# Rotary exchanges issued by ScalarE instead of SyncE, and the solve's plain blocks recorded ahead of the transposed ones, in a two-layer hybrid decoder trunk

## The chip, the cores and the metric

One core of one Trainium2 chip. The metric is device time in microseconds; lower is better. PE is TensorE, DVE is VectorE, ACT is ScalarE, POOL is GpSimd, SP is SyncE; SPq is the sequence in which SP issues DMAs.

## The reference

Two layers over 512 tokens of width 1024. Each layer has a token mixer of four head groups that read one normalised input through one combined projection, then cross-attention into 256 memory tokens, then a SwiGLU FFN. Two of the head groups matter here:

```python
def rotary(x, cos, sin):
    half = x.shape[-1] // 2
    x1, x2 = x[..., :half], x[..., half:]
    ...
    return jnp.concatenate([x1 * c - x2 * s, x1 * s + x2 * c], axis=-1)

# retention group
qh = rotary(heads(q), cos, sin)
kh = rotary(heads(k), cos, sin) * (HEAD_DIM ** -0.5)

# RWKV-7 group, per token
sa = jnp.einsum('bhvk,bhk->bhv', state, -kk_t)
state = (state * w_t[:, :, None, :] + sa[..., None] * (kk_t * a_t)[:, :, None, :]
         + v_t[..., None] * k_t[:, :, None, :])
```

The kernel takes the RWKV recurrence 64 tokens at a time, which needs the inverse of a unit triangular 64x64 matrix for each head and each 64 tokens.

## The kernel before

Channels lie on the partitions and the 512 tokens along the free dimension. Every large product is done with a high and a low part of each operand: a weight block of 1024x128 is loaded by SP into one of three buffers `u`, ACT rounds it into `v` (CAST v<-u), DVE takes the rest into `w` (w<-u,v), and PE makes 24 matmuls of 128x128 by 128x512 into an accumulator `a`. These are called dense matmuls below. All other products go into the five PSUM tiles `b`. SBUF tiles `s` are 128x512, there are 71; `z` and `q` are smaller tiles of the RWKV scan. `fd` and `nd` are tensors in DRAM.

**What sets the order.** The program is first only recorded. `Sched.record` notes each operation with its operands, and links it to what it depends on; `Sched.order` then simulates the five engines with a table of costs (`Sched.cost`: a DMA that SP or ACT issues holds its engine 470 ns) and takes, again and again, the operation that can start first, with ties broken by class and by the length of the chain behind it. The instructions are issued in that order, so each engine has a fixed sequence, and the waits are semaphores. The trace gives all operations line 564, the line in `Sched.issue` that calls them, so places are named by tiles. Moving a DMA to another engine, or recording it earlier, lets the planner come to another order for all that follows.

**The solve** (`rwkv_solve`, one per layer). POOL inverts the 32x32 diagonal blocks by substitution into `rf`, with one block per partition. ACT then makes a transposed copy: `A.copy(rt, rf.rearrange("p t w -> p w t"))`. Both are stored to DRAM (`fd..0` from `rt`, `fd..1` from `rf`; two DMAs each), and read back by 16 DMAs of 32 KB into four block-diagonal tiles: two from `rf` (called TT, one for each pair of heads) and two from `rt` (called R). `rwkv_whole` then makes the 64x64 inverses for each pair: 16 small matmuls of 64x64 with TT, a mask on DVE (two halves, `s<-b,cst`), 16 small matmuls with R, and a sum on DVE that puts the result in R. After both pairs, the scan over eight pieces of 64 tokens begins; its first product with R is the row `b<-z,s`.

**The rotary exchanges** (`retention`). Four projections per layer, q and k of two head pairs each, are rotated. For each, ACT copies the accumulator to `c`; four DMAs of 32x512 exchange neighbouring groups of 32 partitions from `c` into `s`; DVE multiplies the accumulator by the cosines into `t`, multiplies `s` by the sines and adds the two:

```python
A.copy(c, ps)
for b in range(4):
    o = 32 * (b ^ 1)
    self.Q.dma_start(s[o:o + 32], c[32 * b:32 * b + 32])
V.tensor_tensor(t, ps, rot[0], op=ALU.mult)
V.tensor_tensor(s, s, rot[1], op=ALU.mult)
V.tensor_tensor(t, t, s, op=ALU.add)
```

`self.Q` is SP. In the trace the exchange is `s<-s` on SPq. The solve and the rotary are independent of each other, and the planner interleaves both with the projections, the SSD group and later the RWKV scan.

Of the kernel before, what the change touches and what calls it, by code (L numbers as in the profile page):

```python
# [566 lines left out]
class Trunk:  # L567
# [468 lines left out]
    def retention(self, l, proj, vals):  # L1036
        V, A, E, G = self.V, self.A, self.E, self.G
        ident = self.con("ident")
        rot = []
        for i in range(2):  # L1040
            t = self.S()
            self.Q.dma_start(t, self.a["rot"][i])
            rot.append(t)
        qk = []
        for which in range(2):
            for i in range(2):
                ps = proj(COL_B + 256 * which + i * P)
                t, s, c = self.S(), self.S(), self.S()
                A.copy(c, ps)
                for b in range(4):  # L1050
                    o = 32 * (b ^ 1)
                    self.Q.dma_start(s[o:o + 32], c[32 * b:32 * b + 32])
                V.tensor_tensor(t, ps, rot[0], op=ALU.mult)
                V.tensor_tensor(s, s, rot[1], op=ALU.mult)
                V.tensor_tensor(t, t, s, op=ALU.add)
                qk.append(t)
        q, k = qk[0:2], qk[2:4]
        yt = rot
        st = None
        for j in range(4):  # L1060
            tk = slice(j * P, (j + 1) * P)
            v, ks = vals[j], self.S()
            b = self.bank()
            for i in range(2):
                E.transpose(b[:, i * P:(i + 1) * P], k[i][:, tk], ident)
            V.tensor_tensor(ks[:, 0:256], b[:, 0:256], self.con("retw"), op=ALU.mult)
            m = self.S()
            m4 = m.rearrange("p (i o t) -> p i o t", i=2, o=2)
            for o in range(2):
                b = self.bank()  # L1070
                rows = slice(HD * o, HD * o + HD)
                for i in range(2):
                    E.matmul(b[:, i * P:(i + 1) * P], k[i][rows, tk], q[i][rows, tk], start=True, stop=True)
                V.tensor_tensor(m4[:, :, o], b[:, 0:256].rearrange("p (i t) -> p i t", i=2),
                                self.con("retd").rearrange("p (i o t) -> p i o t", i=2, o=2)[:, :, o], op=ALU.mult)
            if j:
                for i in range(2):
                    V.tensor_tensor(q[i][:, tk], q[i][:, tk], self.con("retq")[:, i * P:(i + 1) * P], op=ALU.mult)
            yb = self.bank()
            for i in range(2):  # L1080
                if j:
                    E.matmul(yb[:, i * P:(i + 1) * P], q[i][:, tk], st[:, i * P:(i + 1) * P], start=True, stop=False, skip_group_check=True)
                for h in (2 * i, 2 * i + 1):
                    E.matmul(yb[:, h * HD:(h + 1) * HD], m[:, h * P:(h + 1) * P], v[:, h * HD:(h + 1) * HD],
                             start=(j == 0), stop=True, skip_group_check=True)
            A.copy(yt[j // 2][:, j % 2 * 256:(j % 2 + 1) * 256], yb[:, 0:256])
            if j < 3:

                for i in range(2):
                    E.matmul(yb[:, (2 + i) * P:(3 + i) * P], ks[:, i * P:(i + 1) * P], v[:, i * P:(i + 1) * P], start=True, stop=True)  # L1090
                new = ks[:, 256:512]
                V.tensor_tensor(new.rearrange("p (i c) -> p i c", i=2), yb[:, 256:512].rearrange("p (i c) -> p i c", i=2),
                                self.con("bones").unsqueeze(1).to_broadcast([P, 2, P]), op=ALU.mult)
                if j:
                    for i in range(2):
                        hs = slice(i * P, (i + 1) * P)
                        V.scalar_tensor_tensor(new[:, hs], st[:, hs], self.con("retg")[:, i:i + 1], new[:, hs], op0=ALU.mult, op1=ALU.add)
                st = new
        for t in yt:
            self.head_norm(t, 1e-5)  # L1100
        yy = []
        for i in range(2):
            b = self.bank()
            for j in range(4):
                E.transpose(b[:, j * P:(j + 1) * P], yt[j // 2][:, j % 2 * 256 + i * P:j % 2 * 256 + (i + 1) * P], ident)
            A.activation(k[i], b, AF.Identity, bias=self.par("ret_gn_b", l, i), scale=self.par("ret_gn_w", l, i))
            yy.append(k[i])
        return yy
# [103 lines left out]
    def rwkv_solve(self, l, nd):  # L1212


        V, A, G = self.V, self.A, self.G
        B, H = 32, 16
        nf = self.s.tile("n").rearrange("p (s t) -> p s t", s=B)
        rf = self.S().rearrange("p (t w) -> p t w", w=H)
        room = nf.rearrange("p s t -> p (s t)")
        rt = room[:, 0:B * H].rearrange("p (w t) -> p w t", t=B)  # L1220
        blk = [(self.rows(e).start + B * kb, e * HD + B * kb, B * kb) for e in range(2) for kb in range(HD // B)]
        for c2 in range(2):
            for m, (p0, x0, c0) in enumerate(blk):
                f0 = HD * c2 + 16 * m
                self.Q.dma_start(nf[f0:f0 + 16], nd[p0:p0 + B, :, x0:x0 + B].rearrange("s n t -> n s t"))
        flat = rf.rearrange("p t w -> p (t w)")
        G.memset(flat, 0.0)
        for c2 in range(2):
            G.memset(flat[HD * c2:HD * c2 + HD, H * c2:B * H:2 * H + 1], 1.0)
        for s in range(B - 1):  # L1230
            a, w = B - 1 - s, s // 2 + 1

            p0 = 0 if s else B * (B - 1)
            p3 = room[:, p0:p0 + a * w].rearrange("p (a w) -> p a w", a=a)
            G.tensor_tensor(p3, nf[:, s, s + 1:].unsqueeze(2).to_broadcast([P, a, w]),
                            rf[:, s, 0:w].unsqueeze(1).to_broadcast([P, a, w]), op=ALU.mult)
            done = G.tensor_tensor(rf[:, s + 1:, 0:w], rf[:, s + 1:, 0:w], p3, op=ALU.add)
        A.copy(rt, rf.rearrange("p t w -> p w t"))
        res = [[], []]
        for k, f in enumerate((rt, rf)):  # L1240
            fd = self.s.scratch([HD, B, B], f"fd{l}{k}", True)
            for c2 in range(2):
                half = fd.rearrange("f (w c) t -> f w c t", c=2)[:, :, c2] if k == 0 else fd[:, :, H * c2:H * c2 + H]
                self.Q.dma_start(half, f[HD * c2:HD * c2 + HD])
            for i in range(2):
                t = self.S()
                self.s.link(done, V.memset(t, 0.0), False)
                t3 = t.rearrange("p (n x) -> p n x", n=8)
                for m, (p0, x0, c0) in enumerate(blk):
                    f0 = 16 * m + 8 * i  # L1250
                    self.Q.dma_start(t3[p0:p0 + B, :, c0:c0 + B], fd[f0:f0 + 8].rearrange("n s t -> s n t"))
                res[i].append(t)
        self.solved = done
        return res

    @staticmethod
    def rows(e):
# [456 lines left out]
```

## Time and profile before

| | before |
|---|---|
| median of 3 runs | 1683.56 us (1681.34 to 1685.95) |
| the profiled execution, device time | 1683.98 us |
| its span, first to last instruction | 1682.1 us |
| PE busy | 1643.6 us (98%) |
| DVE busy | 1015.1 us (60%) |
| ACT busy | 633.2 us (38%) |
| mean granted clock of TensorE | 0.992 |

The span is split in the profile into 40 slices of 42 us; PE is at nine tenths or more in nearly all of them, and the slices that are not lie at the start, around 160 us, around 980 us, and at the end. The two in the middle are the solves of the two layers. A timeline row merges neighbouring like instructions: start, length, engine, operation, operands, count, and in brackets the idle time before it and what ended that. A granted clock of 1.00 is 2.4 GHz, one of 0.50 is 1.2 GHz.

### The profile page before, as it was taken

To read this page: it belongs to the slowest core of one execution; us is meant where nothing else is said; L and a number is where in the kernel's file an instruction comes from. 1 tells how busy PE (TensorE), PEld (TensorE's weight loads), DVE (VectorE), ACT (ScalarE), POOL (GpSimd) and SP (SyncE) were. 2 spreads that over 40 slices of the span, in tenths; PEclk is the share of its full clock that TensorE was granted. 3 is DMA by queue.
4 is the path that set the end of the run, shared out by engine and by line. 5 is a ranking of instruction groups with operands and counts; after the bars stand their busy time and mean duration, and the time that the engine had idled before them with its cause. 6 is when DMAs were issued, how large, how long until landed. Compare 5 with 4: busy or idle time off the path is not lost.

```text
span 1682.1 us, 21417 instructions
## 1 busy us (share of the span) xinstructions
PE 1643.6 (98%) x8344; PEld 1344.0 (80%) x8344; DVE 1015.1 (60%) x1796; ACT 633.2 (38%) x966; POOL 69.6 (4%) x140
## 2 busy tenths in 40 slices
PE   7998999999999999999999989999999999999997
PEld 7786778888788888888888867888888888888886
DVE  8867689666564545533477666986655655554333
ACT  7433246444442322322354332554444323232221
POOL 0043000000000000000000700000000000000001
PEclk9999999999999999999999999999999999999998
DMA  9345112632323333333453431145233333333331
GB/s 287 103 101 126 26 45 81 189 94 66 97 88 99 89 100 90 95 104 114 131 175 101 107 83 45 51 126 162 64 88 88 100 89 99 93 96 94 92 97 57
DMA packets 312900, 169.48 MB, mean 101 GB/s; under 512 B 35936, under 2 KB 300384, under 8 KB 312672
## 3 DMA queue, kind: packets, MB, share of 16 engines
q1 hardware_dynamic: 312800, 168.12, 34.8%
q8 instruction: 66, 1.08, 0.3%
q14 instruction: 34, 0.28, 0.1%
HBM read 156.56 MB, written 9.44 MB: 99 GB/s over the span
## 4 chain that ended last, share of the span: by engine, by line
PE 91%; DVE 4%; DMA 2%; ACT 2%; SPq 1%; issue 1%; DVEq 0%; ACTq 0%
PE a L564 81%; PE b L564 9%; DVE s L564 2%; ACT s L564 1%; DMA s<-s 1%; DVE w L564 1%; SPq L564 1%; ACT v L564 1%; DMA s<-in_lora_dram 0%; DMA s<-fd 0%; DMA s<-in_memT_dram 0%; DVE q L564 0%; DVE t L564 0%; DVEq L1710 0%; DVE z L564 0%
## 5 line engine op out<-in xcount | busy, mean ns | idle before, releaser
L564 PE MATMUL a<-s,v 128*128 128x512 f32 (+1 forms) x4012 | 1234.0, 388 | 7.6 <-ACT s L564 5.9
L564 PEld LDWEIGHTS a<-s,v 128*128 128x128 f32 x4012 | 743.8, 189 | 168.2 <-ACT s L564 6.5
L564 PE MATMUL a<-s,w 128*128 128x512 f32 (+1 forms) x2006 | 777.2, 387 | 0.5 <-DVE w L564 0.5
L564 ACT CAST v<-u 128x1024 fp32r<-128x1024 f32 (+3 forms) x275 | 282.4, 1027 | 673.6 <-PE a L564 384.4
L564 PEld LDWEIGHTS a<-s,w 128*128 128x128 f32 x2006 | 378.8, 189 | 80.0 <-issue 0.9
L564 DVE TENSOR_TENSOR w<-u,v 128x1024 fp32r<-128x1024 f32 (+3 forms) x275 | 329.2, 1198 | 169.5 <-ACT v L564 168.8
L564 DVE TENSOR_TENSOR s<-a,s 128x512 f32<-128x512 f32 (+1 forms) x132 | 90.5, 689 | 264.1 <-PE a L564 244.9
L564 ACT ACTIVATE s<-s 128x512 f32<-128x512 f32 (+3 forms) x233 | 144.7, 628 | 111.9 <-DVE s L564 107.3
L564 PE MATMUL b<-s,s 64*64 64x64 f32 (+8 forms) x1268 | 146.0, 275 | 14.8 <-DVE s L564 9.2
L564 DVE TENSOR_TENSOR s<-s,s 128x512 f32<-128x512 f32 (+4 forms) x223 | 139.9, 636 | 30.8 <-DMA s<-s 16.2
L564 PEld LDWEIGHTS b<-s,s 128*128 128x128 f32 (+3 forms) x1268 | 120.9, 171 | 42.9 <-issue 17.3
L564 DVE SCALAR_TENSOR_TENSOR s<-s,s 128x512 f32<-128x512 f32 (+2 forms) x164 | 110.0, 676 | 8.3 <-ACT s L564 7.6
L564 DVE TENSOR_TENSOR s<-s,a 128x512 f32<-128x512 f32 (+1 forms) x49 | 33.2, 677 | 91.8 <-PE a L564 91.8
L564 PE MATMUL a<-v,s 128*128 128x260 f32 (+1 forms) x256 | 67.4, 344 | 0.0
L564 ACT COPY s<-b 64x256 f32<-64x256 f32 (+3 forms) x92 | 30.4, 354 | 80.2 <-PE b L564 74.8
L564 DVE SCALAR_TENSOR_TENSOR s<-s,prm,s 128x512 fp32r<-128x512 f32 (+3 forms) x78 | 52.8, 695 | 4.3 <-ACT s L564 4.2
L564 PE MATMUL b<-cst,s 128*128 128x128 f32 (+2 forms) x312 | 47.9, 266 | 2.3 <-ACT s L564 1.3
L564 PEld LDWEIGHTS a<-v,s 128*128 128x128 f32 x256 | 44.2, 188 | 5.6
L564 PEld LDWEIGHTS b<-cst,s 128*128 128x128 f32 x312 | 38.8, 159 | 11.5 <-DVE s L564 3.9
L564 DVE SCALAR_TENSOR_TENSOR s<-a,prm,s 128x511 f32<-128x511 f32 (+2 forms) x64 | 47.3, 740 | 0.7
L564 ACT CAST s<-s 128x512 fp32r<-128x512 f32 x48 | 29.2, 620 | 45.4 <-DVE s L564 40.4
L564 PE MATMUL a<-w,s 128*128 128x512 f32 (+1 forms) x128 | 43.4, 339 | 0.0
(92 smaller groups left out, 665.8 us busy)
## 6 DMA issues: line engine op xcount, KB each, us to landing
u<-in_ffn_w_in_dram SPq DMA_DIRECT2D x88, 512.0 KB, 3.7
u<-in_w_in_dram SPq DMA_DIRECT2D x52, 512.0 KB, 3.9
u<-in_ffn_w_out_dram SPq DMA_DIRECT2D x32, 512.0 KB, 3.7
u<-in_mem_wv_dram SPq DMA_DIRECT2D x16, 512.0 KB, 3.5
u<-in_w_out_dram SPq DMA_DIRECT2D x16, 512.0 KB, 3.8
u<-in_mem_wq_dram SPq DMA_DIRECT2D x16, 512.0 KB, 3.7
u<-in_mem_wo_dram SPq DMA_DIRECT2D x16, 512.0 KB, 3.7
u<-in_mem_wk_dram SPq DMA_DIRECT2D x13, 512.0 KB, 4.0
```

What stands on the lines that cost most here:

```text
L564: op.fn(*[real(x) for x in op.args], **{k: real(x) for k, x in op.kw.items()})
```

## The change

The four exchange DMAs of a rotary are issued by ACT, behind its copy of the accumulator. In the solve the loop over the two stored forms runs with `rf` first and `rt` second, and the result is turned round so that the caller still gets R before TT.

```diff
                 A.copy(c, ps)
                 for b in range(4):
                     o = 32 * (b ^ 1)
-                    self.Q.dma_start(s[o:o + 32], c[32 * b:32 * b + 32])
+                    A.dma_start(s[o:o + 32], c[32 * b:32 * b + 32])
                 V.tensor_tensor(t, ps, rot[0], op=ALU.mult)
...
         A.copy(rt, rf.rearrange("p t w -> p w t"))
+
         res = [[], []]
-        for k, f in enumerate((rt, rf)):
+        for k, f in ((1, rf), (0, rt)):
             fd = self.s.scratch([HD, B, B], f"fd{l}{k}", True)
...
         self.solved = done
-        return res
+        return [r[::-1] for r in res]
```

How the order moves, in layer 0 (layer 1 reads alike). A name is the tile's kind, a running number and the number of the operation that first wrote it. First SP, from the stores of the solve on. `s_782` is `rf` and `n_774` is `rt`; `s_862`, `s_867` (before) and `s_850`, `s_855` (now) are TT of pairs 0 and 1, the other two R; `s_1700` and `s_1735` are the first two exchanges. Before:

```order
L564 DMA fd_86<-s_782_1087 2048x1x16 x2
L564 DMA fd_85<-n_774_1164 1024x1x32 x2
L564 DMA s_1700_1645<-s_1699_1637 32x512 x2
L564 DMA u_2048_1655<-in_w_in_dram 128x8x128
L564 DMA s_1700_1645<-s_1699_1637 32x512
L564 DMA s_862_1603<-fd_86 32x8x32 x4
L564 DMA s_867_1614<-fd_86 32x8x32 x4
L564 DMA s_850_1619<-fd_85 32x8x32 x4
L564 DMA s_855_1624<-fd_85 32x8x32
...
L564 DMA s_855_1624<-fd_85 32x8x32 x3
L564 DMA s_1700_1645<-s_1699_1637 32x512
L564 DMA s_1735_1798<-s_1734_1781 32x512 x4
```

Now:

```order
L564 DMA fd_85<-s_782_1087 2048x1x16 x2
L564 DMA fd_86<-n_774_1164 1024x1x32 x2
L564 DMA u_2048_1655<-in_w_in_dram 128x8x128
L564 DMA s_850_1603<-fd_85 32x8x32 x4
L564 DMA s_855_1614<-fd_85 32x8x32 x4
L564 DMA s_862_1619<-fd_86 32x8x32 x4
L564 DMA s_867_1624<-fd_86 32x8x32 x2
L564 DMA u_2089_1759<-in_w_in_dram 128x8x128
L564 DMA s_867_1624<-fd_86 32x8x32 x2
```

The exchanges are gone from SP. The stores and reads of the solve stand in the same order in both, `rf` ahead of `rt`.

ACT now, from the first rotary copy's neighbours on (`s_1699` and `s_1734` are the first two `c`, `s_882` and `s_883` are tiles of the scan, `s_1525`, `s_1530` and `s_1540` belong to the SSD group):

```order
L564 COPY s_882_1658<-b_888_1143 64x256
L564 DMA s_1700_1648<-s_1699_1637 32x512 x2
L564 COPY s_883_1662<-b_884_1138 64x256
L564 COPY s_883_1662<-b_888_1143 64x256
L564 ACTIVATE t_1531_1693<-t_1531_1693 128x4
L564 ACTIVATE s_1530_1703<-b_1521_1684 128x512
L564 COPY s_1540_1713<-b_1534_1699 128x256
L564 ACTIVATE s_1525_1695<-s_1525_1695 128x512
L564 CAST v_1943_1727<-u_1942_1537 128x1024
L564 COPY s_1734_1740<-a_1710_1628 128x512
L564 DMA s_1735_1753<-s_1734_1740 32x512 x4
```

Two issues of the first exchange stand ahead of these rows, between copies of the scan's tiles. Before, the same copies, activations and cast stood there without the DMAs, and the copy to `s_1734` behind them.

DVE in the same place (`s_908` and `s_943` are the masked products of pairs 0 and 1, `s_1704` and `s_1739` the rotary's `t`). Before:

```order
L564 TENSOR_TENSOR s_908_1767<-b_892_1734,cst 128x256 x2
L564 SCALAR_TENSOR_TENSOR s_1548_1776<-s_1354_1358,dpar,b_1544_1764 128x128
L564 COPY s_1540_1710<-b_1550_1774 128x256
L564 TENSOR_TENSOR s_1700_1645<-s_1700_1645,s_1671_1573 128x512
L564 TENSOR_TENSOR s_1704_1634<-s_1704_1634,s_1700_1645 128x512
L564 TENSOR_TENSOR s_943_1812<-b_927_1785,cst 128x256
L564 SCALAR_TENSOR_TENSOR s_1549_1817<-s_1387_1416,dpar,b_1544_1764 128x128
L564 TENSOR_TENSOR s_943_1812<-b_927_1785,cst 128x256
L564 TENSOR_TENSOR s_1735_1798<-s_1735_1798,s_1671_1573 128x512
L564 TENSOR_TENSOR s_1739_1731<-s_1739_1731,s_1735_1798 128x512
```

Now:

```order
L564 TENSOR_TENSOR w_1944_1745<-u_1942_1537,v_1943_1727 128x1024
L564 TENSOR_TENSOR s_1700_1648<-s_1700_1648,s_1671_1573 128x512
L564 TENSOR_TENSOR s_1704_1634<-s_1704_1634,s_1700_1648 128x512
L564 SCALAR_TENSOR_TENSOR s_1548_1774<-s_1354_1358,dpar,b_1544_1742 128x128
L564 COPY s_1540_1713<-b_1550_1768 128x256
L564 SCALAR_TENSOR_TENSOR s_1549_1781<-s_1387_1416,dpar,b_1544_1742 128x128
L564 TENSOR_TENSOR s_908_1789<-b_892_1734,cst 128x256 x2
L564 TENSOR_TENSOR t_1563_1803<-b_1553_1787,t_1321_1677 128x4
L564 TENSOR_TENSOR s_1735_1753<-s_1735_1753,s_1671_1573 128x512
L564 TENSOR_TENSOR s_1739_1736<-s_1739_1736,s_1735_1753 128x512
...
L564 TENSOR_TENSOR s_943_1856<-b_927_1809,cst 128x256
```

The first rotary's products have moved ahead of pair 0's mask, and the second rotary's ahead of pair 1's.

## Rows read from the trace of the kernel before

**Rows 1.** The page: span, and busy time of PE.
```profile
span 1682.1 us, 21417 instructions
...
PE 1643.6 (98%) x8344; PEld 1344.0 (80%) x8344; DVE 1015.1 (60%) x1796; ACT 633.2 (38%) x966; POOL 69.6 (4%) x140
```
**Rows 2.** Waits of PE, 140-262 and 956-1066 us: total, times, longest, us.
```profile
PE b L564 <- DVE s L564: 4.7, 2, 4.2
...
PE b L564 <- DVE s L564: 4.4, 1, 4.4
```
**Rows 3.** Timeline of PE, single rows in order of time.
```profile
40.22 0.63 PE L564 MATMUL a<-s,v 128*128 128x512 f32 x1 [1.44 <-DVE s L564]
...
167.20 0.57 PE L564 MATMUL b<-s,s 64*64 64x64 f32 x5 [4.18 <-DVE s L564]
...
173.92 0.68 PE L564 MATMUL b<-z,s 64*64 64x64 f32 x8
...
201.01 0.49 PE L564 MATMUL b<-s,s 128*128 128x128 f32 x2 [0.71 <-DVE q L564]
...
982.67 0.29 PE L564 MATMUL b<-s,s 64*64 64x64 f32 x2 [1.13 <-DMA s<-fd]
...
1000.24 0.67 PE L564 MATMUL b<-z,s 64*64 64x64 f32 x8
...
1043.16 0.91 PE L564 MATMUL b<-s,s 128*128 128x128 f32 x6 [1.17 <-DVE q L564]
```
**Rows 4.** Timeline of DVE, layer 0.
```profile
156.60 1.21 DVE L564 TENSOR_TENSOR w<-u,v 128x1024 fp32r<-128x1024 f32 x1
...
158.33 0.74 DVE L564 TENSOR_TENSOR s<-b,cst 128x256 f32<-128x256 f32 x2
...
164.75 1.42 DVE L564 TENSOR_TENSOR s<-s,s 128x512 f32<-128x512 f32 x2 [4.53 <-DMA s<-s]
```
**Rows 5.** Timeline of SP's DMA issues, layer 0.
```profile
143.91 3.21 SPq L564 DMA_DIRECT2D fd<-s  x2
...
151.96 7.49 SPq L564 DMA_DIRECT2D s<-fd  x13
...
159.98 1.56 SPq L564 DMA_DIRECT2D s<-fd  x3
161.59 32.52 SPq L564 DMA_DIRECT2D s<-s  x7
...
194.78 1.25 SPq L564 DMA_DIRECT2D s<-s  x2
```
**Rows 6.** Stretches: length, busy of PE, PEld, DVE, ACT, POOL; granted clock, DMA share, GB/s.
```profile
40.00:41.00 1.00, 0.79 (x2) 0.67 (x3) 1.00 (x3) 0.41 (x1) 0.00 (x0) 0.71 0.99 317
...
43.00:44.00 1.00, 1.00 (x4) 0.81 (x4) 1.00 (x3) 0.00 (x0) 0.00 (x0) 0.58 1.01 357
...
166.00:168.00 2.00, 0.80 (x15) 0.83 (x17) 1.09 (x4) 0.00 (x0) 0.00 (x0) 0.68 0.47 113
...
172.00:174.00 2.00, 2.00 (x10) 1.65 (x11) 0.41 (x2) 0.00 (x0) 0.00 (x0) 0.61 0.00 0
```
**Rows 7.** Timeline of ACT, layer 0.
```profile
148.72 0.59 ACT L564 COPY s<-a 128x512 f32<-128x512 f32 x1 [0.99 <-DVE s L564]
...
150.39 1.96 ACT L564 COPY s<-b 64x256 f32<-64x256 f32 x6 [0.55 <-DVE s L564]
...
153.39 0.60 ACT L564 ACTIVATE s<-b 128x512 f32<-128x512 f32 x1 [1.04 <-DVE t L564]
...
155.06 1.05 ACT L564 CAST v<-u 128x1024 fp32r<-128x1024 f32 x1
156.00 0.63 ACT L564 ACTIVATE s<-s 128x512 f32<-128x512 f32 x1
```
**Rows 8.** The page: DMA issues, KB each, median us to landing.
```profile
s<-s SPq DMA_DIRECT2D x32, 64.0 KB, 2.0
```
**Rows 9.** The chain that ended last: the longest run of dense matmuls.
```profile
479.07 365.96 PE a L564 x1591
```

## The prediction

> **What bounds the kernel now.** I read the page first: PE is busy 1643.6 of 1682.1 us [rows 1], so a change that leaves PE's work alone can only win back part of 38 us, and only where PE stands still or runs slowly. Then the waits of PE, stretch by stretch. Most idle time lies at the start and the end, which the change does not reach. The longest wait inside is the same in both layers, 4.2 and 4.4 us, for a DVE result [rows 2]: PE stops in the middle of the 64x64 inverses and goes on at 167.20 [rows 3]. Then DVE's timeline, to see why: it stood 4.53 us before a product whose operand came by an `s<-s` DMA [rows 4]. That is the first rotary's exchange. The mask for pair 1, on which PE hangs, has nothing to do with the rotary; it stands behind that product on DVE. Last SP's timeline: the fourth part of the exchange was issued at 161.59, though its source was copied by 149.3 [rows 5, 7]. Between them SP issued the 16 reads of the solve, 9 us.
>
> The wait costs more than its length. Behind it the granted clock falls to the lower level, 1.2 GHz: 0.68 in 166 to 168, 0.61 in 172 to 174 and 0.50 between [rows 6], which is 6.8 us at half clock (1.3 + 4 + 1.5), some 6.4 of them with PE busy, so 3.2 us of lost work. Layer 1 shows the same.
>
> **The change part by part.**
>
> *The solve's order.* Costs nothing and gives nothing: SP's sequence already had `rf` stored and read ahead of `rt`, and it has so still. The planner goes by readiness, not by the order of recording. Only names of buffers are swapped.
>
> *SP loses 32 issues.* Two took 1.25 us [rows 5], so one takes 0.6 and all 20 us. SP is not on PE's path by itself; what counts is the 161.59.
>
> *ACT gains 32 issues.* ACT issues no DMA before, so no row has the price. Nearest are the same DMAs on SP, 0.6 us; the dearest DMA of this place is a store of the solve, 3.21 / 2 = 1.6; the floor is nothing. I take 0.6, as it is the same transfer.
>
> Now I walk through layer 0 in the new order, with durations of before. ACT: copy done 149.3; two copies of scan tiles, 149.8; two issues, 151.0; four copies at 1.96 / 6 = 0.33, 152.3; two issues, 153.5; two copies, 154.1; the SSD group's short steps, 0.2 to 0.63 each, 155.9; cast 1.05, 157.0; second rotary copy 0.59, 157.6; four issues, 160.0; landed 2.0 later [rows 7, 8], **162.0**. The first exchange, whose last issue ends at 153.5, has landed by 156.
>
> DVE starts its next block of work when ACT's last activation is there, 155.9: product 0.7, cosine product 0.7, `w` 1.21, at 158.6; the first rotary's two products 1.42 [rows 4] with no wait, 160.0; three SSD steps, 161.0; mask of pair 0, 0.74, **161.7**; the second rotary's products at 162.0, to 163.4; three SSD steps, 164.3; mask 0.4, R of pair 0 0.7, mask 0.4, 165.8.
>
> PE meets pair 0's mask at 161.9, having waited about 1.5 us (its other rows there end at 160.3) and some 1.2 us earlier for an SSD operand at 156.9. From 161.9 come 32 small matmuls with four dense between them, to 165.0, seven dense, 166.6, two SSD products, 167.0; pair 1's last 16 with one dense, 168.2; the scan's first sums and five dense, 169.7. DVE has R of pair 1 at 169.1, then 0.34 and 0.43 for `z`. The first product with R starts at **170.0**, against 173.92 [rows 3]. By then PE's sequence has 21 of the next dense matmuls behind it, before it had 10; 11 x 0.23 [rows 9] is 2.5 us of work taken out of what follows. Gain in layer 0: 3.9 + 2.5 = **6.4 us**, at the full clock.
>
> Layer 1: the inverses began at 982.67, after a 1.13 us wait for the reads; three exchange issues no longer stand ahead of these, but a read also waits for the slowest store, so I give 0.4 for that. 982.3 + 14.5 (170.0 - 155.5, from the first small matmul to the first product with R) is 996.8, against 1000.24: 3.4; ten dense more, 2.3; **5.7 us**.
>
> *The clock.* Does it fall again? A wait of 1.44 us at 40.22 was followed by half clock from 40.4 to 43.8 (0.71, 0.50, 0.50, 0.58), while 1.13 at 982.67 was not [rows 3, 6]. The new waits, 1.2 and 1.5 us with three busy us between them, look most like the first. That fall lasted 3.4 us, 3.2 of them busy, and cost 1.6. I take 1.6 in each layer; the ends are 0 and the 3.2 of now.
>
> *Later exchanges.* The third and fourth of a layer ran behind SP's weight loads and made waits of 0.71 (layer 0) and 1.17 (layer 1) on PE [rows 3]. They may go, or others come: 0, with 1.9 as the good end.
>
> *ACT's load.* 16 x 0.6 = 9.6 us more per layer on an engine that is busy 38%. The third group ends 0.9 us before the scan's next copy is due, by the same walk, the fourth has as much room; so it is hidden at this price.
>
> *What is late next.* After the exchange it is DVE itself: the weight's low part, the rotary products and pair 0's mask, one behind the other. The solve's last read is not: it lands by about 164, and pair 1's second product starts at 167.0.
>
> Sum: 6.4 + 5.7 - 1.6 - 1.6 = **8.9 us**. The profiled execution took 1683.98 us, 0.4 above the median of the runs; 1683.98 - 8.9 is **1675**. Good end: no fall of the clock and the later waits gone, 14.0, 1670. Poor end inside this mechanism: the clock falls as long as now, 5.7, 1678.3.
>
> **The rivals.** A measurement of this kernel can tell about 0.3%, 5 us, from no change.
>
> *The issues are slower side by side.* ACT's second group is issued while SP is still issuing reads, at 7.49 / 13 = 0.58 each. If the two take turns, each of ACT's four issues waits up to 0.45 to 0.58 more, the exchange lands 1.8 to 2.3 later, and in the new order R of pair 0 and pair 1's mask stand behind its product. Some 1.8 us per layer comes back: 8.9 - 3.6 = 5.3, **1678.7**. For it: the new order has put pair 1's mask behind a later exchange than before. Against: the reads may be over by then. The Trainium skill ("Perfetto Trace Analysis", section on the HWDGE DMA instruction) says that the generator of descriptors is shared between sequencers and locked while one uses it, and that the lock wait is part of the reported duration; by that rule this rival would be the outcome. No run here has two engines issuing, so no row shows it yet.
>
> *The wait moves to the reads.* Semaphores of DMAs are dealt out in turn, so an SP read may now wait for one of ACT's exchanges and the other way round. If pair 1's last read thereby lands at 168 instead of 164, pair 1's product starts a microsecond later than in my walk and the clock falls as now: gain 2 to 3 us in all, **1681**, no measurable change. Against: in the walk there are 3 us to spare.
>
> *Slower: ACT's issues hold the scan.* On ACT the second group stands ahead of the scan's start and the third and fourth ahead of the copies of `u` by which the scan goes from one piece to the next. At a price p each layer is late by 12 x (p - 0.6) less about 1.8 of room. The gain of some 4.5 per layer is used up at p = 1.1 us. At 1.6, the dearest DMA row here, it is 12 - 1.8 = 10.2 late per layer: 2 x (10.2 - 4.5) = 11, **1695**. For it: the planner reckons 0.47. Against: the same DMA took 0.6 on SP.
>
> **How the numbers follow.** Forecast (1672 to 1677.5) 0.47; the clock stays up, 1670 to 1672, 0.13; slower issues or a long fall of the clock, 1677.5 to 1680, 0.20; the wait moves, 1680 to 1687, 0.12; ACT holds the scan 0.08. Faster by over 5 us means below 1678.5: 0.47 + 0.13 + half of 0.20 = 0.70. Within it: 0.10 + 0.12 = 0.22. Slower 0.08. The range 1669.5 to 1681 takes in the first three and a little of the fourth.
>
> **What would show it.** Right: no `s<-s` wait over 1 us on DVE near 160 and 985; the rows `b<-z,s` at about 170 and 997; PE's longest wait there under 2 us. DMA issues on ACT of about 0.6 us. Clock: one short stretch at 0.50, or none. Wrong: issues on ACT over 1 us, a wait of ACT on a DMA before a copy of `u`, or a PE wait of 4 us that names the reads, the mask or the second exchange.

## The result, and the profile after

The changed kernel takes **1667.35 us** (median of 4 runs, 1666.93 to 1668.33) against 1683.92 (1681.34 to 1685.95): ratio 0.9898, 95% interval 0.9884 to 0.9913. That is 16.6 us less. The prediction was 1675 with a range from 1669.5, so the direction was right and the size only a little over half; 1667.35 lies below the range.

The page of the changed kernel, its span and busy times, answers to [rows 1]. PE does the same 8344 matmuls in 8 us less busy time, because less of it runs at half clock:

```profile
span 1665.1 us, 21424 instructions
...
PE 1635.5 (98%) x8344; PEld 1336.9 (80%) x8344; DVE 1014.1 (61%) x1796; ACT 634.7 (38%) x966; POOL 69.2 (4%) x140
```

Where the time came from is read from stretches (length, busy of PE, PEld, DVE, ACT and POOL with their counts, then granted clock, DMA share, GB/s). Before: the start, the solve of layer 0, the solve of layer 1.

```profile
40.00:45.00 5.00, 4.79 (x14) 3.36 (x15) 5.00 (x9) 2.07 (x4) 0.08 (x1) 0.66 0.98 331
...
155.00:180.00 25.00, 19.65 (x212) 15.24 (x210) 14.10 (x34) 4.70 (x11) 0.00 (x0) 0.86 0.25 52
...
975.00:1005.00 30.00, 22.95 (x226) 17.83 (x226) 16.62 (x41) 7.91 (x21) 0.00 (x0) 0.89 0.41 83
```

After, the same work (layer 1 comes 9 us earlier):

```profile
40.00:45.00 5.00, 4.39 (x18) 2.95 (x18) 4.97 (x9) 2.44 (x4) 0.28 (x1) 1.00 0.93 309
...
155.00:180.00 25.00, 24.57 (x261) 19.02 (x261) 18.79 (x48) 6.71 (x15) 0.00 (x0) 1.00 0.35 80
966.00:996.00 30.00, 27.52 (x274) 21.29 (x272) 22.09 (x56) 9.82 (x23) 0.00 (x0) 1.00 0.49 104
```

Layer 0: PE idles 24.57 - 19.65 = 4.9 us less, and the 6.4 us that it worked at half clock, 3.2 us of lost work, are gone; 0.3 of these 8.1 goes again into small waits of the scan, 7.8 remain. Layer 1: 4.6 of idle time, and 5.9 us worked at half clock, 2.9 of lost work; 7.5, and with the scan 7.8. The last 1.0 us comes from the start. By the start of the same dense matmul, the profiled execution of now is 0.5 us ahead of that of before at 40 us and 1.0 ahead at 46; between the two, before had the clock down and this one had not. All 16 profiled executions (before, now and e1 to e14) have the same sequence on every engine until 145 us, by tile names and shapes, and six of them show such a fall between 40 and 46 us and ten do not. So this part is not the change's. 7.8 + 7.8 + 1.0 = 16.6, of the 17.0 by which the two profiled spans differ (1682.1 - 1665.1); that the medians differ by 16.6 as well is chance.

PE's timeline in the two solves answers to [rows 2, 3]. The waits of 4.18 and 4.43 us are gone; the first product with R stands at 169.98 and 988.91:

```profile
160.08 0.64 PE L564 MATMUL b<-s,s 64*64 64x64 f32 x10 [0.21 <-DVE s L564]
...
169.98 0.67 PE L564 MATMUL b<-z,s 64*64 64x64 f32 x8
...
973.27 0.29 PE L564 MATMUL b<-s,s 64*64 64x64 f32 x2 [1.14 <-DMA s<-fd]
...
988.91 0.68 PE L564 MATMUL b<-z,s 64*64 64x64 f32 x8
```

DVE's timeline, layer 0, answers to [rows 4]: the first rotary's two products start at 156.90 without a wait, pair 0's mask follows at 159.27. A wait is left before the second rotary's products, 1.51 us, and nobody on PE hangs on it (the bracket names a read of the solve, which had used the same completion semaphore as the exchange's last part):

```profile
156.90 1.41 DVE L564 TENSOR_TENSOR s<-s,s 128x512 f32<-128x512 f32 x2
...
159.27 0.75 DVE L564 TENSOR_TENSOR s<-b,cst 128x256 f32<-128x256 f32 x2
...
161.60 1.42 DVE L564 TENSOR_TENSOR s<-s,s 128x512 f32<-128x512 f32 x2 [1.51 <-DMA s<-fd]
```

The issues on ACT, and between them ACT's copies (compare [rows 7]):

```profile
147.71 0.59 ACT L564 COPY s<-a 128x512 f32<-128x512 f32 x1 [0.99 <-DVE s L564]
148.19 0.37 ACT L564 COPY s<-b 64x256 f32<-64x256 f32 x1
148.32 0.59 ACTq L564 DMA_DIRECT2D s<-s  x1
148.45 0.37 ACT L564 COPY s<-b 64x256 f32<-64x256 f32 x1
148.95 0.59 ACTq L564 DMA_DIRECT2D s<-s  x1
...
151.12 0.64 ACT L564 COPY s<-b 64x256 f32<-64x256 f32 x2 [0.24 <-DVE t L564]
...
156.50 3.48 ACTq L564 DMA_DIRECT2D s<-s  x4
...
175.06 2.44 ACTq L564 DMA_DIRECT2D s<-s  x4
```

and on SP (compare [rows 5]):

```profile
149.57 11.20 SPq L564 DMA_DIRECT2D s<-fd  x14
160.87 0.41 SPq L564 DMA_DIRECT2D u<-in_w_in_dram  x1
161.31 1.07 SPq L564 DMA_DIRECT2D s<-fd  x2
```

ACT's third group takes 2.44 / 4 = 0.61 us per issue. ACT's second group, beside SP's reads, takes 0.87 each, and SP's reads 11.20 / 14 = 0.80, where they took 0.58 before. But the length of a row takes in the waits between its issues. SP waited here for exchanges of ACT to land (total, times, longest, us; SP, 149 to 163):

```profile
SPq L564 <- DMA s<-s: 3.1, 2, 2.1
```

Without these, (11.20 - 3.1) / 14 = 0.58 is left, as before. In layer 1 ten reads and ACT's second group stand side by side at 0.53 and 0.61 each:

```profile
972.59 5.32 SPq L564 DMA_DIRECT2D s<-fd  x10
...
975.43 2.44 ACTq L564 DMA_DIRECT2D s<-s  x4
```

### The profile page after: what moved, and what is told of

The parts are those of the page before. It is cut to its first block, busy times and chain, and to the rows that moved or that the text cites. A ratio compares the mean times of both kernels' runs of the same rounds, so it can differ in the third digit from the quotient of the medians.

```text
span 1665.1 us, 21424 instructions
## 1 busy us (share of the span) xinstructions
PE 1635.5 (98%) x8344; PEld 1336.9 (80%) x8344; DVE 1014.1 (61%) x1796; ACT 634.7 (38%) x966; POOL 69.2 (4%) x140
## 3 DMA queue, kind: packets, MB, share of 16 engines
q8 instruction: 66, 1.08, 0.3%
## 4 chain that ended last, share of the span: by engine, by line
PE 91%; DVE 4%; ACT 2%; DMA 1%; issue 1%; ACTq 0%; SPq 0%; DVEq 0%
PE a L564 83%; PE b L564 8%; DVE s L564 3%; ACT s L564 1%; DVE w L564 1%; ACT v L564 0%; DVE t L564 0%; DMA s<-s 0%; DMA s<-fd 0%; DMA fd<-n 0%; DMA s<-in_memT_dram 0%; ACTq L564 0%; DVE z L564 0%; SPq L564 0%; DVE q L564 0%
## 5 line engine op out<-in xcount | busy, mean ns | idle before, releaser
L564 DVE TENSOR_TENSOR s<-s,s 128x512 f32<-128x512 f32 (+4 forms) x223 | 140.7, 638 | 19.3 <-ACT s L564 13.1
L564 PE MATMUL b<-s,s 64*64 64x64 f32 (+8 forms) x1268 | 140.9, 267 | 4.5 <-DVE s L564 1.6
L564 PEld LDWEIGHTS b<-s,s 128*128 128x128 f32 (+3 forms) x1268 | 117.5, 164 | 32.4 <-issue 9.9
```

The costliest lines, as they stand in the source:

```text
L564: op.fn(*[real(x) for x in op.args], **{k: real(x) for k, x in op.kw.items()})
```

## The experiments

**Which half of the change does it?** The exchanges alone, without the new loop in the solve:

```diff
-                    self.Q.dma_start(s[o:o + 32], c[32 * b:32 * b + 32])
+                    A.dma_start(s[o:o + 32], c[32 * b:32 * b + 32])
```

> Only the exchanges go to ACT, the solve's loop is as before. Theory (place in the queue: all of the gain comes from the first rotary exchange of a layer no longer standing behind the solve's reads on SP): 1667.4 within 1 us, the time of the whole change. Rival (the solve's order is worth part of it): 1670 or more.

e1 measured 1668.06 (1667.03 to 1668.85), ratio 0.9877 (0.9846 to 0.9909); each ratio is to the kernel before, run beside it. The loop alone:

```diff
-        for k, f in enumerate((rt, rf)):
+        for k, f in ((1, rf), (0, rt)):
...
-        return res
+        return [r[::-1] for r in res]
```

> Only the solve's loop is turned round, the exchanges stay on SP. Theory: 1683.9 within 2 us, no change from before, with the 4.2 and 4.4 us waits of PE still there. Rival (the solve's order is worth part of it): 1681 or less, with those waits shorter.

e2 measured 1685.01, ratio 0.9992 (0.9971 to 1.0014); the waits of PE are 4.06 and 4.61 us. By tile names and shapes every engine's sequence in e1 is that of the changed kernel, and in e2 that of the kernel before. So the solve's order is worth nothing, as its unchanged sequence on SP said.

**Is it the place in SP's queue?** I thought that whoever issues the exchange, it only has to stand ahead of the reads. The kernel before, with one edit to its finished order (`swap` holds the exchanges in program order, 16 per layer):

```diff
         order = self.order(reserve)
+        swap = [op for op in self.ops if op.bytes and all(isinstance(x, Ref) and x.root.kind == "s" for x in op.args[:2])]
+        for g in (swap[0:4], swap[16:20]):
+            i = min(order.index(op) for op in g)
+            order = [op for op in order[:i] if op not in g] + sorted(g, key=lambda op: op.n) + [op for op in order[i:] if op not in g]
```

> The kernel before in its own order, except that the remaining parts of the first exchange of each layer are issued by SP right behind its first part, ahead of the solve's reads. Theory (place in the queue): the 4.5 and 4.4 us waits of DVE go, PE's 4.2 and 4.4 us and the half clock behind them (3.2 each) go with them, 7.4 to 7.6 per layer, so 1669 to 1671 although ACT issues nothing. Rival (ACT must issue them, or the new order of DVE is what pays): over 1676.

e3 measured 1679.14, ratio 0.9960 (0.9938 to 0.9983). My theory was wrong by 9 us. The wait at the first exchange did go. But others took its place. The last reads are issued until 163.79, 13.4 us after the first rotary copy began (12.8 before), and PE now waits for them until 166.92; before, this wait was hidden behind the longer one for the mask. And DVE waits for the second exchange, which stands behind the reads. PE and DVE of this kernel, layer 0:

```profile
166.92 1.32 PE L568 MATMUL b<-s,s 64*64 64x64 f32 x24 [1.98 <-DMA s<-fd]
```

```profile
168.07 1.42 DVE L568 TENSOR_TENSOR s<-s,s 128x512 f32<-128x512 f32 x2 [3.34 <-DMA s<-s]
```

**Is it the new order, or ACT?** Moving the issues to ACT also made the planner come to another order of everything. Two kernels fill the other corners. The new order, with the exchanges given back to SP at the place that they have in it:

```diff
         order = self.order(reserve)
...
+        for op in swap:
+            op.fn = self.tc.nc.sync.dma_start
```

> The changed kernel's order of everything, but each exchange is issued by SP at the place that it has in that order: two parts ahead of the reads, two among the first four reads, the second exchange among the last. Theory (place in the queue): the first exchange has landed by 156 as in the changed kernel; the reads end up to 2 us later; 1667.5 to 1671. Rival (it takes ACT's own issue, beside SP): the reads delay pair 1 and PE waits 2 us or more again with the clock down, 1676 or more.

e4 measured 1678.47, ratio 0.9945 (0.9918 to 0.9972). The second exchange stands behind fourteen reads there, and DVE waits 6.07 us for it, with pair 1's mask behind it:

```profile
168.47 1.42 DVE L567 TENSOR_TENSOR s<-s,s 128x512 f32<-128x512 f32 x2 [6.07 <-DMA s<-s]
```

And the old order with the exchanges issued by ACT (the same edit in the kernel before, with `scalar` for `sync`):

> The order of the kernel before, unchanged, but each exchange is issued by ACT at the place that it has in that order: the first in time, its fourth part behind the SSD steps, the second behind its copy. Theory C (ACT's issue itself pays: the exchange goes out when its copy is done, and SP's reads are not pushed back): DVE's 4.5 and 4.4 us waits go, the reads end as before or up to 1.5 us later; 1667 to 1672 in the old order too. Theory D (the order that the planner comes to pays, above all the rotary products and SSD steps ahead of pair 0's mask): 1674 or more, with PE waits of 1 us and half clock left around the solve.

e12 measured 1681.65, ratio 0.9971 (0.9951 to 0.9991): theory C fell. No wait of DVE stands at the first exchange any more. Instead SP's last three reads take 4.70 us, where three took 1.56 before [rows 5]:

```profile
162.25 4.70 SPq L567 DMA_DIRECT2D s<-fd  x3
```

The last of them left only at 166.64. SP waits for exchanges to land (total, times, longest, us; SP, 148 to 168):

```profile
SPq L567 <- DMA s<-s: 5.1, 2, 3.2
```

The longer wait is that of the last read: in the trace it waits for the completion semaphore that the first part of the second exchange used last. ACT issued that part at 162.05, 11.7 us after the first rotary copy began, where the changed kernel has 8.8 (156.50 - 147.71). PE waits twice for the reads, and the clock falls behind these waits (0.72 in the mean of 166 to 178):

```profile
167.11 0.30 PE L567 MATMUL b<-s,s 64*64 64x64 f32 x2 [1.69 <-DMA s<-fd]
168.45 1.26 PE L567 MATMUL b<-s,s 64*64 64x64 f32 x22 [1.05 <-DMA s<-fd]
```

So by the medians ACT alone gives 4.1 us, the new order alone 7.5, both 16.6 to 17.9.

**Can SP do it, placed by hand?** The new order on SP again, with SP's list rearranged: first exchange whole and ahead of the reads, second behind twelve reads, third ahead of a weight load that waits for its buffer.

```diff
...
+                if i == first:
+                    out += g[0]
+                if op not in drop:
+                    out.append(op)
+                out += hold.get(op, [])
...
```

> As the run with the changed order on SP, but SP's list is put by hand into the order in which the copies are done: the whole first exchange ahead of the reads, the second behind twelve of the sixteen reads, the third ahead of the weight load that waits for its buffer. Theory A (what counts is when an exchange is issued, not by whom): waits of DVE on s<-s under 1.5 us, 1668 to 1672. Theory B (one queue cannot serve both: 24 issues at 0.58 us are 14 us, and whatever comes last in it is late): PE or DVE waits 1.5 us or more for the reads or the second exchange, and the clock falls, 1674 or more.

e11 measured 1671.99 (1670.07 to 1676.65), ratio 0.9910 (0.9880 to 0.9940), which takes in the 0.9898 of the changed kernel. The time is theory A's, the waits are theory B's: DVE waited 4.70 us for the second exchange in layer 0 and 3.19 in layer 1. In layer 1 that cost nothing against the changed kernel; in layer 0 PE waited 1.09 us for the reads, then 0.58 and 1.13, the clock was down from 170.6 to 177.5, and some 3.7 us were lost. So when an exchange is issued counts for most, and one queue, placed by hand, comes close. That the issuer counts for the rest is seen in this one profile; the times do not show it.

**The planner's guess.** If truer costs made the order, it should get better. First 100 ns for an issue on ACT in place of 470:

```diff
-            op.dur = 1040.0 if op.eng == "POOL" else 470.0
+            op.dur = 1040.0 if op.eng == "POOL" else 100.0 if op.eng == "ACT" else 470.0
```

> The changed kernel, with the planner told 100 ns for an issue on ACT in place of 470 (in the trace ACT's copies go on beside the issues; eight copies and four issues took 4.05 us against 3.63 for the copies alone). The four issues stay together, the order of DVE and PE changes. If a truer cost makes a better order: 1664 to 1667. Rival (it puts the second exchange where its source isn't ready, or pair 0's mask behind it): 1668 to 1680.

e10 measured 1700.11, ratio 1.0085 (1.0067 to 1.0102): with the same DMAs on the same engine the kernel is slower than before, and 33 us slower than the changed one, beyond both expectations. In layer 0, in its ACT sequence an activation that waits 1.66 us for DVE stands between the second copy and its exchange; the exchange goes out at 161.59, DVE waits for it ahead of pair 1's mask, and PE for that, with the clock at 0.57 in the mean of 164 to 180. DVE and PE of this kernel:

```profile
168.60 0.69 DVE L564 TENSOR_TENSOR s<-s,s 128x512 f32<-128x512 f32 x1 [4.66 <-DMA s<-s]
```

```profile
162.88 1.41 PE L564 MATMUL b<-s,s 128*64 128x128 f32 x20 [1.60 <-DVE s L564]
...
170.91 1.21 PE L564 MATMUL b<-s,s 64*64 64x64 f32 x16 [2.74 <-issue]
```

This accounts for layer 0, which is 5 us slower than before. Layer 1 is 11 us slower, with a wait of 2.89 us at 997.47 and one of 2.76 at 1049.15, in the scan (clock 0.72 in the mean of 1030 to 1066); where those come from is open.

Then 1600 ns for each store of the solve:

```diff
+            if op.fine and out.root.kind == "d" and _run(op.args[1]) < 512:
+                op.dur = 1600.0
```

> The changed kernel, with the planner told 1600 ns for each store of the solve (the trace shows 1.6 to 2.3 us) in place of 470. If its order for DVE and PE around the solve is off because it believes the reads too early, the waits there (0.7 and 1.1 us) shrink: 1664 to 1667. Rival (they hang on the landing of the stores, not on the order): 1667 to 1670.

e9 measured 1668.18, ratio 0.9902 (0.9879 to 0.9925), no difference from the changed kernel, and there could be none. The condition asks for pieces of under 512 bytes in the source (`op.args[1]`), but there each partition's row of a store of the solve is one piece of 2048; only the target is in small pieces. So no operation got the new cost, and the program is the changed kernel's. e9 is the changed kernel once more, and neither expectation was tested. It did not help to give the stores of the transposed copy to ACT:

```diff
-                self.Q.dma_start(half, f[HD * c2:HD * c2 + HD])
+                (A if k == 0 else self.Q).dma_start(half, f[HD * c2:HD * c2 + HD])
```

> The changed kernel, with the two stores of the transposed copy issued by ACT too, so that SP comes to the reads 1.7 to 1.9 us of issue time earlier. If PE's wait for the reads in layer 1 (1.1 us) hangs on SP's place, it goes: 1665 to 1666.5. Rival (the reads wait for the stores to land, or the stores hold ACT ahead of the rotary copy): 1667 to 1672.

e8 measured 1676.81, ratio 0.9936 (0.9918 to 0.9953). The 1.1 us wait in layer 1 went (to 0.60, for ACT), but the planner's order changed with it: in layer 0 ACT issues the second exchange 10.5 us after the first rotary copy began instead of 8.8, and the clock falls again, for 10 us.

**What does an issue on ACT cost?** The third and fourth exchange of each layer as twice as many DMAs, in the same order:

```diff
...
+                if op in swap:
+                    for h in (slice(0, 16), slice(16, 32)):
+                        op.fn(*[real(x[h]) for x in op.args])
+                    continue
```

> The changed kernel, with the third and fourth exchange of each layer issued as eight DMAs of 16 rows instead of four of 32, in the same order: 16 more issues on ACT per kernel, 4 x 4 of 0.61 us. The prediction's rival (ACT's issues hold the scan; 1.8 us of room per layer at 0.6 each): 4.9 us more of ACT's time per layer, so 3 us late per layer, 1673. Theory (the issues lie in ACT's idle time, 3.5 and 3.3 us ahead of the next row in the changed kernel): 1667 to 1669.

e5 measured 1683.03 (1680.0 to 1685.63), ratio 0.9974 (0.9956 to 0.9991), against 0.9898 of the changed kernel: 0.0076 of 1684 is 12.8 us, more than either expectation. ACT issues for 5.00 us in a row, the copies behind are late, and PE waits 1.76 and 2.99 us in layer 0, with half clock after each. PE of this kernel:

```profile
181.59 1.19 PE L570 MATMUL b<-s,s 128*128 128x128 f32 x10 [1.76 <-ACT s L570]
...
205.94 0.76 PE L570 MATMUL b<-z,s 64*64 64x64 f32 x8 [2.99 <-DVE z L570]
```

The changed kernel's 2.44 us just fit.

**What does the clock cost?** The prediction charged 1.6 us per layer for a fall of the clock behind a wait of 1.4 us. In the changed kernel I had the first half of a mask done over again on DVE, `extra[op]` times, which computes the same:

```diff
...
-                op.fn(*[real(x) for x in op.args], **{k: real(x) for k, x in op.kw.items()})
+                for _ in range(1 + extra.get(op, 0)):
+                    op.fn(*[real(x) for x in op.args], **{k: real(x) for k, x in op.kw.items()})
```

> The changed kernel, with the first half of pair 1's mask done over again on DVE, 10 times more in layer 0 and 14 times in layer 1 (0.34 us each; PE has about 1.9 us to spare): PE should wait some 1.5 us in layer 0 and 2.9 us in layer 1. By the prediction's rule (a wait of 1.4 us is followed by half clock for some 3.4 us) the clock falls in both and each layer loses its wait plus 1.6 or more. Rival (a single wait of this length does nothing to the clock): granted clock 1.00 in layer 0, and the loss is the wait alone.

> The same with 18 in layer 0 and 7 in layer 1: waits of some 4.2 us and 0.5 us. Both theories: half clock behind the first, as in the kernel before, for 6 to 7 us; 1.00 behind the second.

The waits came out longer than meant. e6 (1681.48, one run): 3.83 us in layer 0 and 5.65 in layer 1, each with half clock behind it for 6.8 us. e7 (1687.41, one run): 7.49 in layer 0, half clock until 186, and 2.45 in layer 1, where it lasted from 1002 to 1012. PE of e7 in layer 1 and two stretches behind it:

```profile
1001.40 1.09 PE L567 MATMUL b<-s,s 64*64 64x64 f32 x20 [2.45 <-issue]
```

```profile
1002.00:1004.00 2.00, 2.00 (x23) 1.33 (x19) 0.07 (x1) 0.00 (x0) 0.00 (x0) 0.50 0.00 0
1010.00:1012.00 2.00, 2.00 (x15) 1.68 (x15) 0.96 (x2) 0.80 (x1) 0.00 (x0) 0.50 0.03 8
```

In the same layer a wait of 1.22 us at 985.83 was followed by a short fall from 988 to 992 (0.57 and 0.58, some 1.7 us of work). So the length of the fall does not go with that of the wait. Then the waits that the prediction had in mind, first at pair 1's mask (e13, 5 and 4 times), then at pair 0's (e14, 3 times in both layers):

> The changed kernel, with the first half of pair 1's mask done over again 5 times in layer 0 and 4 times in layer 1. From the two runs before (waits of 2.45, 3.83, 5.65 and 7.49 us at 7, 10, 14 and 18 times) PE should wait 1.5 us and 1.1 us. The prediction's rule for the clock (such a wait costs 1.6 us of half clock behind it): 1667.4 + 1.5 + 1.6 + 1.1 + 1.6 = 1673 within 1 us, with half clock for about 3.4 us. Rival (the clock either stays, or falls for 5 us or more as in the kernel before): no fall, 1670; with one fall of 5 to 10 us, 1672.5 to 1675; with two, 1675 to 1680.

> The changed kernel, with the first half of pair 0's mask done over again 3 times in both layers, so that PE waits there about 1.5 us as the prediction's walk had it (0.21 in the changed kernel), and with the later masks 1.4 us later too. If the walk's wait had come, the prediction says what it costs: 1.3 + 1.6 per layer, 1673. Rival (no fall of the clock behind a wait of this length at this place): the wait alone, 1670. Rival (a fall as long as before's): 1675 to 1680.

e13 measured 1672.47 (1671.38 to 1673.14), e14 1671.41 (1669.82 to 1673.41). In the profiles PE waits 1.53 and 1.08 us, then 1.59 and 1.58, and the clock does not fall. PE of the second in layer 0, and the stretch behind:

```profile
162.26 0.64 PE L567 MATMUL b<-s,s 64*64 64x64 f32 x10 [1.59 <-DVE s L567]
```

```profile
164.00:170.00 6.00, 6.00 (x80) 4.59 (x78) 2.92 (x8) 0.60 (x1) 0.00 (x0) 1.00 0.21 52
```

The profiled executions lie near the low end of their runs. The mean granted clock is 0.996 in all four runs of e13, so the others lost no more than some 2 us to it; in e14 it is 0.995 in the slowest run (1673.41) and 0.997 in the profiled one, so more of that run went at half clock; where is not shown.

No kernel tried is faster than the changed one beyond the noise.

## Why the prediction was wrong in size

The mechanism was right: the exchange waits behind the reads, DVE behind the exchange, and PE behind DVE, with half clock after it. Two steps of the sum failed. The term for the clock, -1.6 in each layer, measured 0: the two waits of PE that it hung on, 1.2 and 1.5 us, measured 0.2 at most. And the terms for the layers, 6.4 and 5.7, measured 7.8 and 7.8, because the small matmuls in the work done by the landmark were left out.

**The solve's order costs nothing and gives nothing: right** (e1, e2).

**The wait of DVE goes, and PE's with it: right**, in both layers.

**The walk to 170.0: right in its landmark, wrong in what it stands for.** The row stands at 169.98, and since the first rotary copy PE made 37 dense matmuls where it had made 26, the eleven that were counted. But this execution was 1.0 us ahead already at that copy (147.71 against 148.72), so the stretch took 22.3 us against 25.2 before, a gain of 2.9 and not 3.9; that the landmark came out to 0.02 us is luck. And "11 x 0.23 is 2.5 us of work taken out of what follows" left out the small matmuls: worked out at full clock, PE did 21.1 us of work in the stretch against 19.75 - 3.2 = 16.5, 4.6 more. 2.9 + 4.6 is 7.5, where the prediction had 6.4. The term for layer 1 was short by more, 5.7 against 7.8; its walk was copied from the other. There the stretch from the first small matmul to the first product with R gained 1.9 us (17.57 to 15.64) where the prediction had 3.4, but PE did 15.2 us of work in it against 13.1 - 2.9 = 10.2, 5.0 more where it had 2.3. The wait for the reads ahead of it, off which the prediction took 0.4, stayed (1.13 before, 1.14 now).

**The two new waits of PE, 1.2 and 1.5 us: wrong.** They were 0.2 at most. The walk laid ACT's four issues end to end with its copies. In the trace they run beside them: from the start of the rotary copy to the end of the eight small copies ACT took 4.05 us (147.71 to 151.76), against 5.4 in the walk (148.7 to 154.1) and 3.63 in the kernel before, without issues (148.72 to 152.35 [rows 7]). DVE was done with pair 0's mask at 160.0, where the walk had 161.7, or 160.7 when this execution's head start is taken off. PE had other work until 159.9.

**The clock, -1.6 in each layer: wrong, 3.2 us.** The clock did not fall. The waits that were to bring it down did not come, and the price was read from one row: a wait of 1.44 at 40.22 with a fall behind it [rows 3, 6]. All 16 profiled executions have this wait, 1.43 or 1.44 us, in the same place and behind the same instructions; six have the fall and ten, the changed kernel among them, have not. And e14 has waits of 1.58 and 1.59 with none; e7's 1.22 had one. A single row was not enough to make a term of.

**Issues on ACT at 0.6: right** (0.61), beside SP's reads in layer 1 too.

Sum: 8.9 predicted; 3.2 for the clock, 1.4 and 2.1 for the two layers and 1.0 for the start of the profiled execution make 16.6.

**The rivals.** *Issues slower side by side* is not what the trace shows. In layer 1 ACT's four issues beside SP's reads take 0.61 each, as when SP is quiet, and the reads 0.53. In layer 0 the longer rows hold 3.1 us of waits for exchanges to land. 26 issues of both queues between 148.32 and 162.38 are 0.54 us each with these waits in them; on SP alone in e4 26 took 150.62 to 166.49, 0.61 each. The Trainium skill ("Perfetto Trace Analysis", section on the HWDGE DMA instruction) says that the sequencers share the generator and that the wait for its lock is part of the duration; layer 1 shows no such lengthening. One issue of ACT's second group in layer 0 took 1.6 us, beside slow ones of SP, but before, with SP alone, one read took 1.4. *The wait moves to the reads* is what the old order on ACT shows (e12). Its mechanism, a read that waits for an exchange's semaphore, is in the changed kernel too, with the 3.1 us: its last read is issued by 162.38, 14.7 us after the first rotary copy began, later than before (12.8) and than in e3 (13.4). PE has no wait for it, because in the new order other rows come first: PE is at pair 1's last product at 167.52, 19.8 us after that copy, where e12 had waited for it until 168.45, 18.1 after. The second exchange also goes out 2.9 us earlier after the copy than in e12. "The solve's last read lands by about 164" was too early as well: in e3 it is 3.1 us from the end of the last issue to PE's start. *ACT holds the scan* has its break-even: 1.1 us per issue was reckoned, and with twice the issues, 1.22 us for each 32 rows, in the third and fourth group alone, 12.8 us of the gain are gone (e5).

**The cause as the runs show it.** Not the engine and not the place alone. SP has one list for reads that wait for stores and for exchanges that wait for ACT, and whatever stands last in it is late (e3, e4); put in order by hand, the list costs little (e11). A second queue takes the exchanges out of that list. The Trainium skill ("DMA: Bandwidth & Descriptors", section "Issuing engines are not separate DMA queues") says that this saves only the time on the sequencer, which is usually small beside the transfer; here that time is what counts, 26 issues of 0.61 us in one row. It paid in full only in an order in which the second rotary's copy comes early, so that its exchange lands before the last reads need a semaphore and DVE waits for it only 1.51 us, and in which PE comes late to pair 1's last product (e12, layer 0 of e10).

## What to carry to other kernels

When a DMA that hangs on a compute engine shares a queue with a long row of others, issue it from the engine that makes its source: it then goes out when the copy is done. Then look what has moved: with a planner, an edit of who issues is an edit of the whole order, and here that was worth more (1667 to 1700 us with the same DMAs on the same engine) than the issue itself; a run of the old order on the new engine and one of the new order on the old engine tell them apart. Count all work that an engine has done by a landmark, the small instructions too, and make no term of a clock fall out of a single row.

## What was not expected of the hardware

ACT issues a DMA while its copies run on: four issues of 0.5 to 0.6 us made nine copies only 0.4 us longer. SP's reads wait for exchanges that ACT issued, because both queues use the same completion semaphores: 3.1 us in layer 0 of the changed kernel, 5.1 in e12. Half clock, where it came behind a wait, lasted 3.4 us (behind 4.06 in e2 and 1.76 in e5), 6.8 (behind 3.83 and 5.65 in e6), 10 (behind 2.45 in e7, and in e3 in layer 1 behind 0.81 and 0.78 close together) or 17 (behind 7.49 in e7), while single waits of 1.58 had none and one of 1.22 had 3.4 us. Why the clock falls at 42 us in some executions and not in others, behind the same wait, is open.
